# In the projections' stage of a two-layer trunk: rotation and weights' low parts from GpSimd to VectorE, decay weights and scan in fewer operations

## The chip, the cores and the metric

One core of one Trainium2 chip runs the whole kernel in one launch. The metric is device time in microseconds (us); the profile is one execution of the program, and its "span" is what the trace covers of it. Engines are named as in the profile: PE (TensorE), DVE (VectorE), ACT (ScalarE), POOL (GpSimd), SP (SyncE, which issues nearly all DMAs).

## The reference, cut to what matters

Two layers over 1024 latent tokens and 256 context tokens, D = 1024, all fp32. Each layer normalises and modulates its input, multiplies it by one wide input projection, and feeds three head groups: a Conformer convolution module, a bidirectional chunkwise retention and latent attention. Their outputs are concatenated, projected, and followed by a SwiGLU feed-forward part. The change lies in the retention and the latent heads' inputs:

```python
def _rotate_half_axis(x, pos):
    ...
    x1, x2 = xf[..., :f], xf[..., f:]
    return jnp.concatenate([x1 * cos - x2 * sin, x1 * sin + x2 * cos], axis=-1)

# retention, one chunk:
    o = einsum((q k^T) * dmat, v) + einsum(q, s) * xi
    s = s * g_chunk + einsum(k * zeta, v)
```

Retention's q and k (4 heads of 64) and the latent key's 32 rotary columns are rotated by row and column position, for the 1024 latent tokens only. The convolution has 31 taps over 256 channels.

## The kernel before, in words

Every fp32 matmul is done as three products of a high part (an fp32r rounding, made by ACT) and a low part (the difference, a subtraction in `split`, L80 through the helper `tt`): high by high, low by high, high by low. `piece` loads a 128x1024 piece of weights and splits it; unless told otherwise its low part is made on GpSimd.

The **projections' stage** comes once in each layer (about 146 to 412 us and 1832 to 2074 us of the span). Tokens go in ten tiles of 128: eight latent and two context. `load_chunk` splits the four pieces of a weight matrix, `project` runs 24 matmuls (eight k by three products) into one PSUM bank, and an evacuation follows. There are three passes over the tiles:

- **kv** (`evac_kv`): ACT copies the bank to `kv`, GpSimd rotates the key half (`rope_tm`: one 128x256 product, four 128x64 products, one 128x256 sum), the tile is stored to DRAM, and VectorE makes `kz`, the key times its decay weights in both directions (two operations). Four ticks later (`tk.later`; a tick is two k of a `project`, six matmuls) `states` multiplies `kz` by the values and ACT copies the result to `ST`. After the last tile a scan runs over the ten chunk states (`ST`, nine steps of four operations of 128x64, L660).
- **qg** (`evac_qg`): the same rotation for the query, then the gate (L672), `qx` (query times decay, two operations) and, some ticks later each, `ret_transposes`, `ret_scores` (VectorE multiplies by the decay mask: `AT`), `ret_values` (statistics on VectorE, the power on GpSimd: `rr`, L192) and `ret_store`. The second layer has no context tiles in this pass.
- **c** (`evac_cq`): the latent ranks. VectorE scales them, GpSimd rotates 32 columns, PE transposes them. Here too `conv_norm` normalises the convolution's output.

The 62 **taps** of the convolution (L584, `some_taps`) are VectorE operations of 128x1295 (first layer) or 128x1024 (second layer) elements, two chains of 31. They depend on nothing else in the stage, and only `conv_norm` needs their end. The program is scheduled by a planner that fills each engine's queue in order of emission among what is ready by its own estimate of times. So taps stand wherever VectorE was planned to be free. Once built, each engine's order is fixed: a late instruction holds up all that stand behind it on its engine.

The pools that matter: `kv` has two buffers, `qg` four, `kz` and `qx` share two, the rotation's `m1` and `m2` have one each, the table `rk` two, weights' `wh` and `wl` four each.

Of the kernel before, what the change touches and what calls it, by code (L numbers as in the profile page):

```python
# [11 lines left out]
F32 = mybir.dt.float32  # L12
# [9 lines left out]
T = 1024  # L22
# [6 lines left out]
H_RET = 4  # L29
# [14 lines left out]
def body(tc, I, out):  # L44
    nc = tc.nc
    mult, add, sub = ALU.mult, ALU.add, ALU.subtract
# [32 lines left out]
    def tt(out, a, b, op, eng=None):  # L79
        (eng or nc.vector).tensor_tensor(out=out, in0=a, in1=b, op=op)  # L80

    def split(h, l, t, heng=None, leng=None):

        if heng is None:
            nc.scalar.copy(h, t)  # L85
        else:
            heng.tensor_copy(h, t)
        tt(l, t, h, sub, leng)

    def load(src, n=1024):  # L90
        raw = rawp.tile([128, 1024], F32, name="raw", tag="raw")
        nc.sync.dma_start(out=raw[:, :n], in_=src)
        return raw

    def piece(src, n=1024, heng=None, leng=None, p=None, raw=None):

        raw = load(src, n) if raw is None else raw
        h = (p or whp).tile([128, 1024], F32R, name="wh", tag="wh", bufs=4)
        l = (p or wlp).tile([128, 1024], F32R, name="wl", tag="wl", bufs=4)
        split(h[:, :n], l[:, :n], raw[:, :n], heng, leng or nc.gpsimd)  # L100
        return h, l
# [35 lines left out]
    tk = Ticks()  # L137
# [333 lines left out]
    with ExitStack() as st:  # L471
# [26 lines left out]
        for k in range(KT):  # L498
            t = tp.tile([128, 512], F32, name="ht", tag="ht")
# [10 lines left out]
    for l in range(L):  # L510
# [31 lines left out]
        for g, (o, n) in enumerate(groups):  # L542
            for ct in range(2):
                pp = [bank("mm") for _ in range(2)]
                for hf in range(2):
                    for k in range(KT):
                        wh, wl = apcs[ct][k // 4]
                        c = (k % 4) * 256 + hf * 128
# [5 lines left out]
                        if k % 4 == 3 or k == 1:  # L554
# [4 lines left out]
                                               in1=pp[0][:, :n], op0=add, op1=mult)  # L559
# [11 lines left out]
        ST = rtp.tile([128, 10, 256], F32, name=f"ST{l}")  # L571
        dT, xi, zeta, gC = decay_tables(l, rtp)
        sp = sts.enter_context(pool(f"stage{l}", 2))
# [14 lines left out]
        taps = conv_taps()  # L588

        def load_chunk(name, ncol):  # L590
            return [piece(I[name][l, kp], 2 * ncol) for kp in range(4)]

        def project(pcs, ncol, t):

# [10 lines left out]
        def rope_tm(p, dst, tab, nh, f):  # L605

            w = 4 * f
            n = nh * w
            m1 = p.tile([128, 256], F32, name="m1", tag="m1", bufs=1)
            m2 = p.tile([128, 256], F32, name="m2", tag="m2", bufs=1)  # L610
            tt(m1[:, :n].rearrange("p (h w) -> p h w", h=nh), dst.rearrange("p (h w) -> p h w", h=nh),
               tab[:, 0:1, :].to_broadcast([128, nh, w]), mult, nc.gpsimd)
            sv = dst.rearrange("p (h b a f) -> p h b a f", h=nh, b=2, a=2)
            mv = m2[:, :n].rearrange("p (h b a f) -> p h b a f", h=nh, b=2, a=2)
            tv = tab[:, 1, :].rearrange("p (b a f) -> p b a f", b=2, a=2)
            for a in range(2):
                for b in range(2):
                    tt(mv[:, :, b, a, :], sv[:, :, b, 1 - a, :], tv[:, b:b + 1, a, :].to_broadcast([128, nh, f]), mult, nc.gpsimd)
            tt(dst, m1[:, :n], m2[:, :n], add, nc.gpsimd)


        fo = {**{t: t + 2 for t in LAT}, 8: 0, 9: 1}
# [3 lines left out]
        def by_head(a):  # L626
            return a.rearrange("p (h d) -> p h d", h=H_RET)

        def evac_kv(t, ps):
            kv = sp.tile([128, 512], F32, name="kv", tag="kv")  # L630
            if t < 8:
                nc.scalar.copy(kv, ps)
                tab = sp.tile([128, 2, 64], F32, name="rk", tag="rk")
                nc.sync.dma_start(out=tab, in_=I["rope_ret"][1, t])
                rope_tm(sp, kv[:, :256], tab, H_RET, 16)
            else:
                nc.scalar.activation(out=kv[:, :256], in_=ps[:, :256], func=AF.Copy, scale=0.125)
                nc.scalar.copy(kv[:, 256:], ps[:, 256:])
            if t in tiles:
                kvd[t] = drp.tile([128, 512], F32, name=f"kvd{l}{t}")  # L640
                nc.sync.dma_start(out=kvd[t], in_=kv)
            kz = sp.tile([128, H_RET, 2, 64], F32, name="kz", tag="kz")
            for i in range(2):
                tt(kz[:, :, i, :], by_head(kv[:, :256]), zeta[:, i, :].unsqueeze(2).to_broadcast([128, H_RET, 64]), mult)
            tk.later(4, states, t, kv, kz)

        def states(t, kv, kz):
            pu = bank("aux")
            for h in range(H_RET):
                nc.tensor.matmul(pu[:, h * 64:h * 64 + 64], lhsT=kz[:, h].rearrange("p a d -> p (a d)"),  # L650
                                 rhs=kv[:, 256 + h * 64:256 + h * 64 + 64], start=True, stop=True)
            if fo[t] < 9:
                nc.scalar.copy(ST[f_, fo[t] + 1, :], pu[f_, :256])
            if bo[t] < 9:
                nc.scalar.copy(ST[b_, bo[t] + 1, :], pu[b_, :256])
            if t == kvt[-1]:
                for i in range(9):
                    for h in range(H_RET):
                        c = slice(h * 64, h * 64 + 64)
                        nc.vector.scalar_tensor_tensor(out=ST[:, i + 1, c], in0=ST[:, i, c], scalar=gC[:, h:h + 1],  # L660
                                                       in1=ST[:, i + 1, c], op0=mult, op1=add)

        def evac_qg(t, ps):
            q = sp.tile([128, 512], F32, name="qg", tag="qg", bufs=4)
            nc.scalar.copy(q[:, :256], ps[:, :256])
            if t < 8:
                tab = sp.tile([128, 2, 64], F32, name="rk", tag="rk")
                nc.sync.dma_start(out=tab, in_=I["rope_ret"][0, t])
                rope_tm(sp, q[:, :256], tab, H_RET, 16)
            th = sp.tile([128, 256], F32, name="thg", tag="thg", bufs=1)  # L670
            nc.scalar.activation(out=th, in_=ps[:, 256:], func=AF.Tanh, scale=0.5)
            nc.vector.scalar_tensor_tensor(out=q[:, 256:], in0=th, scalar=1.0, in1=ps[:, 256:], op0=add, op1=mult)  # L672
            qx = sp.tile([128, H_RET, 2, 64], F32, name="qx", tag="kz")
            for i in range(2):
                tt(qx[:, :, i, :], by_head(q[:, :256]), xi[:, i, :].unsqueeze(2).to_broadcast([128, H_RET, 64]), mult)
            kv = sp.tile([128, 512], F32, name="kv2", tag="kv2", bufs=3)
            nc.sync.dma_start(out=kv, in_=kvd[t])
            tk.later(4, ret_transposes, t, q, qx, kv)
# [143 lines left out]
        for i, t in enumerate(kvt[2:]):  # L822
# [2 lines left out]
                if left:  # L825
                    tk.later(1 + 2 * j, conv_norm, left.pop(0))
            evac_cq(t, project(pcs, 416, t))
        wh, wl = piece(I["w_ukv"][l])
        wq = [piece(I["w_uq"][l, k]) for k in range(2)]
        vd = drp.tile([10, 128, 512], F32, name=f"vd{l}")  # L830

        def values(t_, p):
# [418 lines left out]
        for i, t in enumerate(order):  # L1251
# [8 lines left out]
            x = load_x(w2, t)  # L1260
# [106 lines left out]
        if last:  # L1367
            c = slice(0, 256)
# [8 lines left out]
            c = slice(256, 512)  # L1377
# [4 lines left out]
        else:  # L1382
            c = slice(0, 512)
# [16 lines left out]
        for j in range(NJ):  # L1400
            v = steps.pop(j) if j in steps else first_two(j)
            w, x, u, th1 = v.w, feat.op, v.u, v.th
# [133 lines left out]
        while ahead:  # L1536
            k, n, m, (a_, (bh, bl)) = ahead.pop(0)
            if not last and n in (0, 1, 2, 3):
                ch, cl = ctx[k]
                for t in CTX:  # L1540
                    if n in (0, 1):
                        cps[t] = bank("cx")
                    for i in range(m):
                        c, d, q = slice((t - 8) * 128, (t - 8) * 128 + 128), slice(i * 512, i * 512 + 512), 2 * i + n // 2
# [18 lines left out]
            for t in range(4):  # L1563
                ps = bank("po")
                for i in range(m):
                    c, d = slice(i * 512 + t * 128, i * 512 + t * 128 + 128), slice(i * 512, i * 512 + 512)
# [32 lines left out]
        for t in tiles:  # L1599
# [8 lines left out]
            for i, hf in inner:  # L1608
                wh, wl = pcs[i]
                d = slice(hf * 512, hf * 512 + 512)  # L1610
# [10 lines left out]
            x = load_x(e3, t)  # L1621
# [17 lines left out]
def _tables():  # L1639

    row, col = np.arange(T) // 64, np.arange(T) % 64

    def tab(f):
        cr, sr = _rope(row, f)
        cc, sc = _rope(col, f)
        return np.concatenate([cr, cr, cc, cc], 1), np.concatenate([-sr, sr, -sc, sc], 1)

    c16, s16 = tab(16)
    c8, s8 = tab(8)
    ret = np.stack([c16, s16], 1).reshape(8, 128, 2, 64)  # L1650
    rope_ret = np.stack([ret, ret * np.float32(0.125)])
    rope_kr = np.stack([c8, s8], 1).reshape(8, 128, 2, 32)
    rope_q = np.stack([np.tile(c8.T, (4, 1)), np.tile(s8.T, (4, 1))], 1) * np.float32(SCALE)
    m, c = np.arange(128)[:, None], np.arange(128)[None, :]
    posd = np.stack([np.maximum(c - m, 0), np.maximum(m - c, 0)], 1)
    p = np.arange(128)
    posc = np.stack([p + 1, 128 - p, 127 - p, p], 1)
    fold = np.array([[1, 0], [0, 1], [1, 1]])
    return {k: np.ascontiguousarray(v, dtype=np.float32) for k, v in
            dict(rope_ret=rope_ret, rope_kr=rope_kr, rope_q=rope_q, posd=posd, posc=posc, fold=fold).items()}  # L1660
# [67 lines left out]
```

## Time and profile before

| | us |
|---|---|
| median of three runs | 3169.01 (3164.75 to 3169.87) |
| profiled execution, its time | 3160.68 |
| span of its trace | 3158.9 |
| kv pass, qg pass, c pass of layer 1 in the trace | 146 to 225, 225 to 333, 333 to 412 |
| kv pass, qg pass, c pass of layer 2 | 1832 to 1910, 1910 to 1993, 1993 to 2074 |

How to read it: the profiled execution is one run, 8.3 us under the median of the three timed ones. A table of windows gives, for a stretch of the span, the busy time of each engine; PEclk is the granted clock of TensorE, 1.00 at 2.4 GHz and 0.50 at 1.2 GHz. A list of waits gives whom an engine waited for.

### The profile page before, as it was taken

Reading aid. Unit: us, or ns where it says so; the run is one execution under the profiler, and the core shown is the slowest. Engines: PE = TensorE matmul, PEld = TensorE weight load, DVE = VectorE, ACT = ScalarE, POOL = GpSimd, SP = SyncE. Lnnn points to the kernel's source line nnn. Section 1 sums busy time; section 2 is a strip of 40 time slices with the busy share of each in tenths; the row PEclk is TensorE's granted clock in tenths of the full one; section 3 lists DMA queues with packets and bytes.
Section 4 is the critical chain, followed back from the end, with each engine's and each line's share of the span. In section 5 each row is a group of like instructions: output and inputs, shape, how many; then the busy total and the mean of one; then the engine's idle time right before and its main releaser. Section 6 shows DMA issues by size and latency. Waiting matters only on the chain. (4 is left out here: it accounts for less than half of the span.)

```text
span 3158.9 us, 39704 instructions
## 1 busy us (share of the span) xinstructions
PE 2932.1 (93%) x13968; PEld 2275.9 (72%) x13968; DVE 2306.9 (73%) x3246; ACT 1194.4 (38%) x2354; POOL 1490.8 (47%) x1187
## 2 busy tenths in 40 slices
PE   7989989999889999999898898989999899999997
PEld 3667865567678888887776676875568678887785
DVE  4388568868897766655888868468957976666998
ACT  4223545653422222224332513545544322224432
POOL 1174435644332333226675375436654433334993
PEclk9999999999999999999999999989999999999998
DMA  7421157768522322223303421158864232224213
GB/s 276 143 66 38 46 189 179 179 160 270 172 77 92 105 92 92 98 71 131 112 21 110 153 66 48 44 175 194 198 193 139 97 114 89 82 83 155 98 62 120
DMA packets 178527, 381.47 MB, mean 121 GB/s; under 512 B 43255, under 2 KB 77687, under 8 KB 178072
## 3 DMA queue, kind: packets, MB, share of 16 engines
q1 hardware_dynamic: 172980, 360.03, 37.3%
q10 hardware_dynamic: 5348, 18.90, 1.5%
q8 instruction: 111, 1.82, 0.2%
q14 instruction: 88, 0.72, 0.1%
HBM read 242.97 MB, written 76.90 MB: 101 GB/s over the span
## 5 line engine op out<-in xcount | busy, mean ns | idle before, releaser
L80 POOL TENSOR_TENSOR wl<-raw,wh 128x512 fp32r<-128x512 f32 (+2 forms) x208 | 387.8, 1876 | 657.0 <-ACT wh L85 655.3
L85 ACT CAST wh<-raw 128x512 fp32r<-128x512 f32 (+2 forms) x305 | 237.4, 796 | 412.5 <-PE pp L105 192.9
L80 DVE TENSOR_TENSOR w<-pp,w 128x512 f32<-128x512 f32 x308 | 207.6, 686 | 189.2 <-PE pp L105 187.2
L105 PE MATMUL po<-wh,gh 128*128 128x512 f32 x504 | 203.1, 403 | 34.8 <-DVE p L80 28.2
L990 DVE TENSOR_REDUCE nm<-S 128x1 f32<-128x1280 f32 x128 | 189.7, 1482 | 56.1 <-PE S L105 54.7
L1003 ACT ACTIVATE P<-S,nm 128x1280 f32<-128x1280 f32 x120 | 159.4, 1329 | 176.0 <-DVE nm L990 175.8
L80 POOL TENSOR_TENSOR rr<-rv,mh 128x1 f32<-128x1 f32 (+2 forms) x130 | 93.2, 718 | 275.2 <-DVE rv L190 262.6
L1030 POOL COPY PT<-T 32x1280 f32<-32x1280 f32 x120 | 149.8, 1249 | 117.4 <-PE mm L1015 79.6
L105 PE MATMUL po<-wh,gl 128*128 128x512 f32 x504 | 200.3, 397 | 0.0
L105 PE MATMUL po<-wl,gh 128*128 128x512 f32 x504 | 200.0, 397 | 0.0
L584 DVE SCALAR_TENSOR_TENSOR cacc<-cy,cw,cacc 128x1295 f32<-128x1295 f32 (+1 forms) x120 | 190.1, 1625 | 0.0
L80 POOL TENSOR_TENSOR gl<-gr,gh 128x512 fp32r<-128x512 f32 x112 | 173.9, 1577 | 27.5 <-ACT gh L85 25.8
L80 POOL TENSOR_TENSOR wl<-sx,wh 128x1024 fp32r<-128x1024 f32 x44 | 108.4, 2464 | 157.4 <-ACT wh L85 137.2
L1095 DVE STREAM_TRANSPOSE T<-P 128x1280 f32<-128x1280 f32 x120 | 179.9, 1499 | 0.0
L80 DVE TENSOR_TENSOR raw<-raw 128x512 f32<-128x512 f32 (+1 forms) x96 | 128.2, 1344 | 51.9 <-POOL wl L80 48.5
L1041 PE MATMUL po<-PT,vr 128*64 128x512 f32 x600 | 155.7, 615 | 8.9 <-DVE raw L80 2.2
L105 PE MATMUL S<-kh,qh 96*128 96x512 f32 (+1 forms) x384 | 155.8, 406 | 6.4 <-ACT P L1003 4.4
L80 DVE TENSOR_TENSOR p<-p,po 128x512 f32<-128x512 f32 x224 | 145.3, 677 | 16.6 <-PE po L105 16.1
L105 PE MATMUL S<-kh,ql 96*128 96x512 f32 (+1 forms) x384 | 144.6, 376 | 11.1 <-POOL ql L80 11.0
L105 PEld LDWEIGHTS po<-wh,gh 128*128 128x128 f32 x504 | 97.2, 193 | 65.1 <-DVE p L80 33.2
L80 DVE TENSOR_TENSOR wl<-raw,wh 128x512 fp32r<-128x512 f32 (+1 forms) x105 | 124.4, 1194 | 26.4 <-ACT wh L85 25.0
L105 PE MATMUL S<-kl,qh 96*128 96x512 f32 (+1 forms) x384 | 142.8, 372 | 0.0
(438 smaller groups left out, 8723.6 us busy)
## 6 DMA issues: line engine op xcount, KB each, us to landing
PT<-T SPq DMA_DIRECT2D x360, 160.0 KB
raw<-in_mod_w SPq DMA_DIRECT2D x96, 512.0 KB
raw<-in_ffn_in SPq DMA_DIRECT2D x88, 512.0 KB
gd<-w SPq DMA_DIRECT2D x88, 256.0 KB
gr<-gd SPq DMA_DIRECT2D x32, 512.0 KB
xs<-x ACTq DMA_DIRECT2D x28, 512.0 KB
raw<-in_ffn_out SPq DMA_DIRECT2D x28, 512.0 KB
x<-xs SPq DMA_DIRECT2D x26, 512.0 KB
```

The source lines that it names most:

```text
L80: (eng or nc.vector).tensor_tensor(out=out, in0=a, in1=b, op=op)
L85: nc.scalar.copy(h, t)
L105: nc.tensor.matmul(ps, lhsT=a, rhs=b, start=start and i == 0, stop=stop and i == len(xs) - 1)
L584: nc.vector.scalar_tensor_tensor(out=acc[:, ct, :], in0=y0[:, ct, j:j + AW], scalar=w, in1=acc[:, ct, :], op0=mult, op1=add)
L990: nc.vector.reduce_max(out=u.nm, in_=ps[:, :nk], axis=AX.X, negate=True)
L1003: nc.scalar.activation(out=P, in_=u.ps, func=AF.Exp, bias=u.nm, accum_out=u.sm)
L1030: nc.gpsimd.tensor_copy(o, i)
L1041: nc.tensor.matmul(u.po[64 * (j % 2):64 * (j % 2) + 64], lhsT=u.hd.v[:, j, :], rhs=src[:, :, j * 32:j * 32 + 32], start=j < 2, stop=j > 7)
L1095: nc.vector.transpose(out=T1[:, :, u.a // 128].rearrange("p c (k i) -> p k c i", i=32), in_=u.P.rearrange("p (k c i) -> p k c i", c=4, i=32))
```

## The change

The rotation is done on VectorE in four operations: the source times the cosines, the source times the sines (whose halves are stored swapped in the table), and two sums, one for each half, that take the other half of the second product. It serves kv, qg and, with 32 columns, the c pass. The low parts of `w_kv`, `w_qg`, `w_c`, `w_ukv` and `w_uq` are made on VectorE; all other pieces stay. `kz` and `qx` are one operation of 512 elements each instead of two of 256. The scan's nine steps have two operations of 256 elements each instead of four of 64. `kv` shares the four buffers of `qg`, `kz` gets three, and `states` comes five ticks later instead of four.

```diff
         def load_chunk(name, ncol):
-            return [piece(I[name][l, kp], 2 * ncol) for kp in range(4)]
+            return [piece(I[name][l, kp], 2 * ncol, leng=nc.vector) for kp in range(4)]
...
-            tt(m1[:, :n].rearrange("p (h w) -> p h w", h=nh), dst.rearrange("p (h w) -> p h w", h=nh),
-               tab[:, 0:1, :].to_broadcast([128, nh, w]), mult, nc.gpsimd)
...
+            for i, m in enumerate((m1, m2)):
+                tt(m[:, :n].rearrange("p (h w) -> p h w", h=nh), dst.rearrange("p (h w) -> p h w", h=nh),
+                   tab[:, i:i + 1, :].to_broadcast([128, nh, w]), mult)
+            o, x, y = (a.rearrange("p (g a f) -> p g a f", a=2, f=f) for a in (dst, m1[:, :n], m2[:, :n]))
             for a in range(2):
-                for b in range(2):
-                    tt(mv[:, :, b, a, :], sv[:, :, b, 1 - a, :], tv[:, b:b + 1, a, :].to_broadcast([128, nh, f]), mult, nc.gpsimd)
-            tt(dst, m1[:, :n], m2[:, :n], add, nc.gpsimd)
+                tt(o[:, :, a], x[:, :, a], y[:, :, 1 - a], add)
...
-            kv = sp.tile([128, 512], F32, name="kv", tag="kv")
+            kv = sp.tile([128, 512], F32, name="kv", tag="qg", bufs=4)
...
-            kz = sp.tile([128, H_RET, 2, 64], F32, name="kz", tag="kz")
-            for i in range(2):
-                tt(kz[:, :, i, :], by_head(kv[:, :256]), zeta[:, i, :].unsqueeze(2).to_broadcast([128, H_RET, 64]), mult)
-            tk.later(4, states, t, kv, kz)
+            kz = sp.tile([128, H_RET, 2, 64], F32, name="kz", tag="kz", bufs=3)
+            tt(kz, by_head(kv[:, :256]).unsqueeze(2).to_broadcast([128, H_RET, 2, 64]),
+               zeta.rearrange("p i h -> p h i").unsqueeze(3).to_broadcast([128, H_RET, 2, 64]), mult)
+            tk.later(5, states, t, kv, kz)
...
+                g = gC.unsqueeze(2).to_broadcast([128, H_RET, 64])
                 for i in range(9):
-                    for h in range(H_RET):
-                        c = slice(h * 64, h * 64 + 64)
-                        nc.vector.scalar_tensor_tensor(out=ST[:, i + 1, c], in0=ST[:, i, c], scalar=gC[:, h:h + 1],
-                                                       in1=ST[:, i + 1, c], op0=mult, op1=add)
+                    d = sp.tile([128, 256], F32, name="sd", tag="thg", bufs=1)
+                    tt(by_head(d), by_head(ST[:, i, :]), g, mult)
+                    tt(ST[:, i + 1, :], ST[:, i + 1, :], d, add)
...
-        wh, wl = piece(I["w_ukv"][l])
-        wq = [piece(I["w_uq"][l, k]) for k in range(2)]
+        wh, wl = piece(I["w_ukv"][l], leng=nc.vector)
+        wq = [piece(I["w_uq"][l, k], leng=nc.vector) for k in range(2)]
...
+    def halves_swapped(s):
+        return s.reshape(T, 2, 2, -1)[:, :, ::-1].reshape(s.shape)
...
-    ret = np.stack([c16, s16], 1).reshape(8, 128, 2, 64)
+    ret = np.stack([c16, halves_swapped(s16)], 1).reshape(8, 128, 2, 64)
```

`qx` is changed as `kz` is, and `rope_kr` as `ret` is.

## Rows read from the trace of the kernel before

**Rows 1.** The page's part 1: busy us, share of the span, instructions of each engine.

```profile
PE 2932.1 (93%) x13968; PEld 2275.9 (72%) x13968; DVE 2306.9 (73%) x3246; ACT 1194.4 (38%) x2354; POOL 1490.8 (47%) x1187
```

**Rows 2.** Windows: start:end, us, busy PE, PEld, DVE, ACT, POOL, then PEclk, DMA.

```profile
148.00:320.00 172.00, 151.20 (x748) 121.44 (x746) 144.86 (x220) 44.24 (x109) 108.23 (x108) 0.93 0.18 55
1835.00:1969.00 134.00, 117.40 (x571) 94.16 (x569) 116.57 (x173) 32.11 (x77) 87.45 (x86) 0.95 0.18 57
320.00:367.00 47.00, 45.07 (x285) 40.52 (x286) 22.09 (x78) 27.25 (x85) 20.01 (x37) 1.00 0.20 60
```

**Rows 3.** Waits of PE, 140 to 430 us: us in total, times, longest.

```profile
PE aux L650 <- DVE kz L80: 8.3, 5, 2.5
PE mm L105 <- POOL wl L80: 5.7, 4, 1.9
PE rx L686 <- DVE qx L80: 3.6, 1, 3.6
...
PE ry L683 <- DVE AT L80: 2.1, 3, 1.3
```

**Rows 4.** Waits of PE, 1815 to 2110 us, same columns.

```profile
PE aux L650 <- DVE kz L80: 9.4, 4, 2.6
PE aux L781 <- DVE cq L769: 6.3, 4, 3.5
PE ry L683 <- DVE AT L80: 5.9, 4, 2.8
...
PE mm L105 <- POOL wl L80: 3.3, 2, 1.6
```

**Rows 5.** Timeline of POOL in the kv pass: start, us, instructions.

```profile
198.38 6.69 POOL L80 TENSOR_TENSOR m<-kv,rk 128x256 f32<-128x256 f32 x5 [1.09 <-issue]
```

**Rows 6.** Windows, columns of Rows 2: a PE gap, then stretches at half clock.

```profile
204.80:207.30 2.50, 0.04 (x1) 0.00 (x0) 1.39 (x3) 0.58 (x1) 2.34 (x4) 0.95 0.31 113
...
176.30:179.70 3.40, 3.40 (x11) 2.82 (x11) 3.40 (x3) 0.73 (x2) 3.40 (x3) 0.51 0.34 82
207.10:213.90 6.80, 6.56 (x20) 5.53 (x21) 5.78 (x7) 0.73 (x2) 5.63 (x5) 0.50 0.13 44
251.40:258.20 6.80, 6.80 (x24) 5.24 (x22) 4.27 (x6) 1.89 (x5) 1.38 (x4) 0.50 0.00 0
...
1862.50:1865.90 3.40, 3.40 (x9) 2.66 (x8) 3.25 (x3) 0.21 (x1) 3.32 (x3) 0.50 0.29 88
1900.10:1903.50 3.40, 3.40 (x11) 2.82 (x11) 3.40 (x6) 0.76 (x2) 0.00 (x0) 0.50 0.00 1
1920.60:1927.30 6.70, 6.59 (x20) 5.56 (x21) 6.70 (x18) 1.14 (x3) 4.26 (x4) 0.50 0.03 10
...
2115.10:2142.40 27.30, 27.30 (x73) 20.56 (x73) 23.33 (x17) 13.51 (x19) 14.35 (x11) 0.50 0.67 153
```

**Rows 7.** DVE's groups by shape, 148 to 320 us: busy, mean ns, idle before.

```profile
L584 DVE SCALAR_TENSOR_TENSOR cacc<-cy,cw,cacc 128x1295 f32<-128x1295 f32 x59 | 101.2, 1751 | 0.0
L80 DVE TENSOR_TENSOR kz<-kv,zeta 128x256 f32<-128x256 f32 x20 | 11.3, 608 | 10.4 <-POOL kv L80 10.4
L660 DVE SCALAR_TENSOR_TENSOR ST<-ST,gC 128x64 f32<-128x64 f32 x36 | 9.4, 336 | 0.0
```

**Rows 8.** DVE's groups by shape, 1835 to 1969 us, same columns.

```profile
L584 DVE SCALAR_TENSOR_TENSOR cacc<-cy,cw,cacc 128x1024 f32<-128x1024 f32 x60 | 87.3, 1503 | 0.0
```

**Rows 9.** Instructions on cacc, then kz: ns min/median/max, starts, forms.

```profile
L584 DVE SCALAR_TENSOR_TENSOR cacc<-cy,cw,cacc x120: 1251/1560/3704, 152.0 to 1967.6; 128x1295 f32<-128x1295 f32 x60, 128x1024 f32<-128x1024 f32 x60
...
L80 DVE TENSOR_TENSOR kz<-kv,zeta x40: 412/426/2562, 158.7 to 1920.0; 128x256 f32<-128x256 f32 x40
```

**Rows 10.** DVE elsewhere: a 128-element product (timeline); 512 elements; low parts (groups).

```profile
701.09 0.28 DVE L80 TENSOR_TENSOR od<-od,S 64x128 f32<-64x128 f32 x1 [3.79 <-ACT od L1087]
...
L80 DVE TENSOR_TENSOR w<-pp,w 128x512 f32<-128x512 f32 x308 | 207.6, 686 | 189.2 <-PE pp L105 187.2
...
L80 DVE TENSOR_TENSOR wl<-raw,wh 128x1024 fp32r<-128x1024 f32 x52 | 68.7, 1320 | 12.1 <-ACT wh L85 10.7 <-POOL m_l L80 1.4
```

More of the change, by code (lines that the diff above doesn't have):

```diff
@@ L610, in rope_tm @@
             m2 = p.tile([128, 256], F32, name="m2", tag="m2", bufs=1)
-            tt(m1[:, :n].rearrange("p (h w) -> p h w", h=nh), dst.rearrange("p (h w) -> p h w", h=nh),
-               tab[:, 0:1, :].to_broadcast([128, nh, w]), mult, nc.gpsimd)
-            sv = dst.rearrange("p (h b a f) -> p h b a f", h=nh, b=2, a=2)
-            mv = m2[:, :n].rearrange("p (h b a f) -> p h b a f", h=nh, b=2, a=2)
-            tv = tab[:, 1, :].rearrange("p (b a f) -> p b a f", b=2, a=2)
+            for i, m in enumerate((m1, m2)):
+                tt(m[:, :n].rearrange("p (h w) -> p h w", h=nh), dst.rearrange("p (h w) -> p h w", h=nh),
+                   tab[:, i:i + 1, :].to_broadcast([128, nh, w]), mult)
+            o, x, y = (a.rearrange("p (g a f) -> p g a f", a=2, f=f) for a in (dst, m1[:, :n], m2[:, :n]))
             for a in range(2):
-                for b in range(2):
-                    tt(mv[:, :, b, a, :], sv[:, :, b, 1 - a, :], tv[:, b:b + 1, a, :].to_broadcast([128, nh, f]), mult, nc.gpsimd)
-            tt(dst, m1[:, :n], m2[:, :n], add, nc.gpsimd)
+                tt(o[:, :, a], x[:, :, a], y[:, :, 1 - a], add)
         fo = {**{t: t + 2 for t in LAT}, 8: 0, 9: 1}
@@ L672, in evac_qg @@
             nc.vector.scalar_tensor_tensor(out=q[:, 256:], in0=th, scalar=1.0, in1=ps[:, 256:], op0=add, op1=mult)
-            qx = sp.tile([128, H_RET, 2, 64], F32, name="qx", tag="kz")
-            for i in range(2):
-                tt(qx[:, :, i, :], by_head(q[:, :256]), xi[:, i, :].unsqueeze(2).to_broadcast([128, H_RET, 64]), mult)
+            qx = sp.tile([128, H_RET, 2, 64], F32, name="qx", tag="kz", bufs=3)
+            tt(qx, by_head(q[:, :256]).unsqueeze(2).to_broadcast([128, H_RET, 2, 64]),
+               xi.rearrange("p i h -> p h i").unsqueeze(3).to_broadcast([128, H_RET, 2, 64]), mult)
             kv = sp.tile([128, 512], F32, name="kv2", tag="kv2", bufs=3)
@@ L1646, in tab @@
         return np.concatenate([cr, cr, cc, cc], 1), np.concatenate([-sr, sr, -sc, sc], 1)
+    def halves_swapped(s):
+        return s.reshape(T, 2, 2, -1)[:, :, ::-1].reshape(s.shape)
     c16, s16 = tab(16)
     c8, s8 = tab(8)
-    ret = np.stack([c16, s16], 1).reshape(8, 128, 2, 64)
+    ret = np.stack([c16, halves_swapped(s16)], 1).reshape(8, 128, 2, 64)
     rope_ret = np.stack([ret, ret * np.float32(0.125)])
-    rope_kr = np.stack([c8, s8], 1).reshape(8, 128, 2, 32)
+    rope_kr = np.stack([c8, halves_swapped(s8)], 1).reshape(8, 128, 2, 32)
     rope_q = np.stack([np.tile(c8.T, (4, 1)), np.tile(s8.T, (4, 1))], 1) * np.float32(SCALE)
```

## The prediction

> **What bounds the kernel now.** I read the page's busy times first: TensorE is busy 93% of the span, VectorE 73%, GpSimd 47% [rows 1]. So time is saved where PE stands still or runs slowly, and an edit on another engine counts only through that. Next come windows over the stage, from the first tap of the convolution to the last: 172 us in the first layer, 134 us in the second. PE is idle for 172 - 151.2 = 20.8 us and 134 - 117.4 = 16.6 us of them, at a mean granted clock of 0.93 and 0.95, while VectorE is busy 144.9 and 116.6 us [rows 2].
>
> The waits of PE say for whom it stood. For the key's decay weights (`kz`, L650): 8.3 and 9.4 us. For low parts made on GpSimd: 5.7 and 3.3. For `qx` behind the scan: 3.6, first layer. For `AT` in the retention: 2.1 and 5.9 [rows 3, 4]. `kz` is late because VectorE itself waited 10.4 us for GpSimd's rotated tile [rows 7], and five products of one rotation took 6.7 us there [rows 5]. VectorE stands with its whole queue in such a wait: its order is fixed, and taps behind a waiting `kz` don't move.
>
> The clock windows show a second price. In the gap from 204.8 to 207.3 PE did nothing for 2.5 us; from 207.1 to 213.9 it had 0.50, that is 1.2 GHz. Six such stretches in the two kv passes and starts of the qg passes last 3.4 + 6.8 + 6.8 + 3.4 + 3.4 + 6.7 = 30.5 us [rows 6]. At half speed each loses half its length of matmul work: 15.2 us.
>
> **The change part by part.**
>
> *Rotation of kv.* GpSimd loses six operations per latent tile, VectorE gains four. A 256-element product costs 0.42 us (median of `kz`, same operands) [rows 9], a 128-element one 0.28 [rows 10]: 2 x 0.42 + 2 x 0.28 = 1.4 us against 6.7 and more. No row shows VectorE on runs of 16 elements, as the sums have; I bound a sum by 0.28 below and by 0.42, a full tile's price, above (1.7 us a rotation), and take 0.28, since it has that element count. `kz` follows in the same queue with no wait on another engine. A tap in progress can hold it by up to 1.56 us [rows 9], but `states` now comes one tick, six matmuls, later, and four buffers instead of two keep ACT from waiting for a free `kv`. I take all of the `kz` waits away: 8.3 + 9.4 = **17.7 us**. Ends: nothing (a tap always in the way) and 17.7.
>
> *Low parts.* A piece on VectorE costs 1.32 us [rows 10]. The four `w_kv` pieces fall where taps have not begun, `w_qg` and `w_c` among taps. The waits for GpSimd's low parts go, 5.7 + 3.3 = **9.0 us**; a wait for ACT's high part would be next, and so would a tap ahead of a piece (ends 0 and 9.0).
>
> *Scan and decay weights.* `kz` goes from 2 x 0.608 to one operation of 512 elements, 0.69 [rows 7, 10]; the scan from 9.4 us to 18 x 0.42 = 7.6 us [rows 7, 9]. With `states` one tick later, the scan also comes after the first query tile's evacuation, so `qx` no longer stands behind it: **3.6 us** [rows 3], ends 0 and 3.6.
>
> *Rotation of qg.* It takes the waits for GpSimd out of VectorE's queue, ahead of `AT`, but puts 1.4 us in. Of the 2.1 + 5.9 = 8.0 us for `AT` [rows 3, 4] I give a third back, **2.7 us**; ends: a loss of 8.0 and a gain of 8.0.
>
> *Clock.* If the gaps go, so does most of what follows them. I take three quarters of 15.2: **11.4 us** (ends 0 and 15.2); some gaps of the retention will still throttle.
>
> *VectorE's account.* First layer, 148 to 320 us: 16 rotations of 1.4 and four pieces of 1.32 add 27.7; `kz` saves 11.3 - 10 x 0.69 = 4.4, the scan 1.8. Net +21.5 on 144.9. But a tap takes 1.75 us on average there, 1.56 as a median [rows 7, 9]. I put the difference down to GpSimd reading beside it, and it goes when GpSimd falls silent: 59 x 0.19 = 11.3 us. Left: 155.1 of 172 us, 90%. Second layer, with the same net: 116.6 + 21.5 - 60 x (1.503 - 1.251) = 123.0 of 134 [rows 2, 8, 9]. This cover is thin inside the stretch, but taps are fillers and may run later: from 320 to 367 us VectorE is busy only 22.1 of 47 us [rows 2], and nothing needs the taps before `conv_norm`. If that cover went, the first rival below would hold.
>
> *The c pass.* The 32-column rotation (eight tiles) and three pieces (4.0 us a layer) join a VectorE on which PE already waits: 6.3 us for `cq` in the second layer [rows 4]. Ends: nothing, and that wait doubled in both layers, 12.6. I take **5 us** lost, as VectorE is idle half of the time just before it [rows 2].
>
> *Taps in the way.* Each of 38 kv and qg tiles (20 + 18) may wait up to a tap, 1.56 us: ends 0 and 59. Most have ticks to spare; I take a twelfth, **5 us**.
>
> *Queues.* No DMA is added. SP's stores of `kvd` and loads of `rk` behind them waited for GpSimd's rotation and now wait for a VectorE that ends it sooner; GpSimd's queue keeps only the powers (`rr`), which no longer stand behind rotations. At nothing: both queues run beside PE's matmuls, and if SP were late, the next weight piece would be.
>
> **Sum.** 17.7 + 9.0 + 3.6 + 2.7 + 11.4 - 5 - 5 = 34.4 us. Profiled execution: 3160.7 - 34.4 = 3126.3 us. It lies 8.3 us under the median of the three runs, so against that median, 3169.0, the forecast is **3135 us**.
>
> **The rivals.**
>
> *A. VectorE sets the pace up to the last tap* (no change, or little). For: 90% and 92% by the account above. Its idle time now is 27.1 us (first layer), of which only the 10.4 for `kz` certainly goes; if half of the other 16.7 stays, the stretch takes 155.1 + 8.4 = 163.5, a gain of 8.5. Second layer: idle 17.4, half stays: 131.7, a gain of 2.3. Less 5 for the c pass: about 6 us, **3163 us**. Against: the planner puts taps behind what is due, and they can slide past 320 us. Chance 0.14.
>
> *B. Slower: the rotation stands in front of `AT`.* Place: VectorE's queue in the qg pass, where PE's fixed order waits for each tile's `AT` and `z`. Price: rotation 1.4 and a tap 1.56, 3.0 us a tile, 18 tiles: 54 us lost. Gained on the kv side: 17.7 + 9.0 + three quarters of half of 23.7 us at half clock (all six but the one at 251.4), 8.9. Less 5: 54 + 5 - 35.6 = 23 us slower, **3192 us**. It decides from a lateness of (35.6 - 5) / 18 = 1.7 us a tile on. For: PE waits for `AT` already today [rows 3, 4]. Against: VectorE loses its waits for the rotated query, and a rotation belongs to a tile whose transposes are due four ticks later. Chance 0.08. The Trainium skill (Perfetto Trace Analysis, Identifying the Most-Contended Engine) has a rule on this side: improve the engine with the highest occupancy first; the change loads VectorE, which has the higher occupancy of the two it concerns. By that rule alone the sum would be the account's net, some 20 us a layer lost; the waits of PE, mostly for GpSimd's work, speak against it here.
>
> *C. More than forecast.* From 2115 to 2142 us PE runs 27.3 us at half clock [rows 6], at the door of the second layer's attention. If the stage ends otherwise, that may vanish too: 13.6 us more, about **3121 us**. Against: a gap just ahead of it is none that the change touches. Chance 0.14.
>
> That the change does not do what it says is hardly a case: engine, shape and count of each operation are given.
>
> **How the numbers follow.** Forecast 0.64, with its own range of 3122 to 3150 from the ends of clock, `AT` and tap costs; A 0.14, B 0.08, C 0.14. The time is that of the likeliest case. The range reaches to C below, with some of the upper ends of the gains (3110), and to A above (3164); left out are B, half of A, and little below. About 0.2% (6 us) is what a measurement can tell from no change: half of A lies within it. Faster: 0.64 + 0.14 + 0.07 = 0.85; same 0.07; slower 0.08.
>
> **What would show it.** Right: PE's waits for `kz` and for low parts nearly absent; kv pass shorter by 10 to 15 us in each layer; taps near 1.56 and 1.25 us on average; fewer than three half-clock stretches in kv and qg together; GpSimd nearly empty there. A shows as a VectorE without idle time and a first `conv_norm` that waits for the last tap; B as PE's waits for `AT` and `z` above 30 us. Rotations above 2 us each would make the account wrong, and with it the forecast.

## The result, and the profile after

The change makes the kernel **81 us faster**: 3087.89 us (3084.57 to 3096.54, four runs) against 3169.09, a ratio of 0.9753 [0.9739, 0.9767] (in brackets a 95% interval, here and below). The direction was forecast, the size was not: the gain is more than twice the 34.4 us of the sum, and the time lies below the range. The profiled execution has a span of 3082.8 us, 76.1 less than before; it lies 3.3 us under its own median, the one of before 8.3 under its own, and 76.1 + 8.3 - 3.3 = 81.1. All executions compared here have a mean granted clock of 0.96 to 0.98; one of an added-work kernel below, at 0.567 and 4722.68 us, is left out.

Part 1 of the page after answers to [rows 1]:

```profile
PE 2896.8 (94%) x13968; PEld 2252.0 (73%) x13968; DVE 2318.9 (75%) x3394; ACT 1196.4 (39%) x2354; POOL 1240.9 (40%) x869
```

VectorE carries only 12 us more than before, though GpSimd has given up 250. PE's own busy time fell by 35 us with the same 13968 matmuls, and its mean granted clock rose from 0.969 to 0.979.

Where the time went is read best between events that both kernels have. These windows run from ACT's first copy of a `kv` tile to its last copy of a `qg` tile, and from there to the last copy of a transposed key at the end of the c pass, for both layers; columns as in [rows 2]. Before:

```profile
152.70:332.40 179.70, 159.16 (x813) 128.72 (x813) 147.56 (x236) 53.53 (x130) 110.02 (x110) 0.93 0.18 55
332.40:445.80 113.40, 104.92 (x567) 90.55 (x566) 59.53 (x164) 55.79 (x172) 48.57 (x90) 0.97 0.35 117
1838.40:1992.10 153.70, 135.69 (x697) 109.52 (x696) 122.81 (x204) 44.83 (x106) 97.56 (x102) 0.96 0.17 54
1992.10:2104.90 112.80, 100.22 (x529) 86.72 (x529) 56.51 (x152) 52.54 (x163) 49.03 (x92) 0.97 0.33 109
```

And after:

```profile
148.40:291.90 143.50, 143.50 (x810) 120.18 (x808) 132.38 (x259) 53.55 (x130) 10.08 (x7) 1.00 0.22 69
291.90:404.80 112.90, 104.07 (x572) 88.54 (x572) 77.20 (x211) 56.20 (x172) 31.85 (x37) 1.00 0.34 115
1799.10:1923.30 124.20, 124.20 (x689) 104.10 (x687) 114.89 (x228) 45.47 (x106) 6.38 (x5) 1.00 0.20 65
1923.30:2030.40 107.10, 99.51 (x538) 84.83 (x538) 68.54 (x200) 52.84 (x163) 26.38 (x33) 1.00 0.34 114
```

In kv and qg PE is now busy in every microsecond by the profile, at full clock (1.00): 143.50 of 143.50 and 124.20 of 124.20. The two stretches are 36.2 and 29.5 us shorter, the c passes 0.5 and 5.7. With the 4.3 us by which the first window starts earlier, less 1.7 given back between the layers, plus 1.6 after the last window, that is the 76.1.

PE's waits from 140 to 430 us, and (after the dots) from 1765 to 2040, columns as in [rows 3]:

```profile
PE S L105 <- ACT P L1000: 3.1, 3, 1.3
PE ry L792 <- DVE cz L799: 2.9, 7, 1.1
PE ry L792 <- DVE cacc L584: 1.4, 1, 1.4
PE aux L778 <- DVE cq L766: 1.4, 3, 0.6
...
PE ry L792 <- DVE cz L799: 2.2, 5, 0.9
PE aux L778 <- DVE cq L766: 1.7, 2, 0.9
...
PE ry L680 <- DVE AT L80: 0.4, 1, 0.4
```

All that [rows 3, 4] showed for `kz`, low parts, `qx` and `AT` is gone but 0.4 us. What is left belongs to the c pass and the attention. Line 3 is the last tap: the first `conv_norm` waited 1.4 us for it.

VectorE's groups from 144 to 292 us answer to [rows 7]:

```profile
L584 DVE SCALAR_TENSOR_TENSOR cacc<-cy,cw,cacc 128x1295 f32<-128x1295 f32 x49 | 76.3, 1560 | 0.1
L80 DVE TENSOR_TENSOR kz<-kv,zeta 128x512 f32<-128x512 f32 x10 | 6.9, 686 | 1.6 <-ACT kv L634 1.4
...
L80 DVE TENSOR_TENSOR m<-kv,rk 128x256 f32<-128x256 f32 x16 | 6.1, 421 | 0.9 <-ACT kv L629 0.9
L80 DVE TENSOR_TENSOR wl<-raw,wh 128x1024 fp32r<-128x1024 f32 x5 | 6.0, 1219 | 0.2 <-ACT wh L85 0.2
...
L80 DVE TENSOR_TENSOR kv<-m,m 128x128 f32<-128x128 f32 x16 | 3.9, 284 | 0.0
```

A tap takes 1.56 us instead of 1.75, a product of the rotation 0.42, a sum on runs of 16 elements 0.28, and the 10.4 us that VectorE stood for GpSimd's tile are gone. This window holds ten taps fewer than that of [rows 7] (49 against 59): they slid behind 292 us.

### The profile page after: what moved, and what is told of

It reads as the page before. It is cut to its first block, busy times and chain, and to the rows that moved or that the text cites. A ratio compares the mean times of both kernels' runs of the same rounds, so it can differ in the third digit from the quotient of the medians.

```text
span 3082.8 us, 39513 instructions
## 1 busy us (share of the span) xinstructions
PE 2896.8 (94%) x13968; PEld 2252.0 (73%) x13968; DVE 2318.9 (75%) x3394; ACT 1196.4 (39%) x2354; POOL 1240.9 (40%) x869
## 5 line engine op out<-in xcount | busy, mean ns | idle before, releaser
L80 POOL TENSOR_TENSOR wl<-raw,wh 128x512 fp32r<-128x512 f32 (+1 forms) x178 | 310.9, 1758 | 550.1 <-ACT wh L85 550.0
L105 PE MATMUL po<-wh,gh 128*128 128x512 f32 x504 | 203.3, 403 | 33.5 <-DVE p L80 24.4
L80 DVE TENSOR_TENSOR wl<-raw,wh 128x1024 fp32r<-128x1024 f32 (+2 forms) x135 | 158.9, 1185 | 46.7 <-ACT wh L85 46.7
L584 DVE SCALAR_TENSOR_TENSOR cacc<-cy,cw,cacc 128x1295 f32<-128x1295 f32 (+1 forms) x120 | 169.5, 1419 | 0.2
L1331 ACT ACTIVATE w<-w 128x512 f32<-128x512 f32 x88 | 55.6, 632 | 220.3 <-DVE w L80 220.3
```

The lines of the kernel that those rows point to most:

```text
L105: nc.tensor.matmul(ps, lhsT=a, rhs=b, start=start and i == 0, stop=stop and i == len(xs) - 1)
L584: nc.vector.scalar_tensor_tensor(out=acc[:, ct, :], in0=y0[:, ct, j:j + AW], scalar=w, in1=acc[:, ct, :], op0=mult, op1=add)
L1331: nc.scalar.activation(out=th, in_=u, func=AF.Tanh, scale=0.5)
```

## The experiments

The texts quoted below name theories by letters. **W**: GpSimd's long rotations make PE's gaps, directly and through VectorE's fixed queue, and the half clock comes behind the gaps. **L**: the low parts are a cause of their own. **S**: the buffers and the later tick are what helps. **P** and **Q**: the small edits matter in combination. **A**: VectorE paces the stage. **C**: GpSimd's work beside VectorE slows both (contention). **D**: only the lateness of GpSimd's results counts.

**One part alone.** First the rotation only, on the kernel of before:

```diff
-            tt(m1[...], dst[...], tab[:, 0:1, :]..., mult, nc.gpsimd)
...
+            for i, m in enumerate((m1, m2)):
+                tt(m[...], dst[...], tab[:, i:i + 1, :]..., mult)
...
+                tt(o[:, :, a], x[:, :, a], y[:, :, 1 - a], add)
```

> Only the rotation moves to VectorE (four operations); low parts, buffers, ticks, decay weights and scan as before. Theory W (PE's gaps come from GpSimd's long rotations, directly and through VectorE's fixed queue, and each gap brings half clock behind it): 45 to 60 us faster than before, PE's waits for kz and AT under 4 us in each layer, taps near 1.56 us on average, and PE's waits for GpSimd's low parts (5.7 and 3.3 us) left. Rival S (kz was late because kv has two buffers and states comes a tick too early): 10 to 25 us faster, kz waits still over 5 us a layer. Rival L (the low parts were the main cost): under 20 us.

Measured: 0.9878 [0.9858, 0.9899], 39 us. PE's waits from 140 to 430 us:

```profile
PE mm L105 <- POOL wl L80: 4.3, 4, 1.9
...
PE aux L647 <- DVE kz L80: 1.3, 1, 1.3
```

`kz` is down from 8.3 to 1.3 [rows 3], the low parts still cost 4.3. The two kv and qg windows are 25.8 and 17.1 us shorter and the c passes 2.8 and 0.7 longer. W's mechanism is there, with less gain than W asked, and one of its signs failed: the mean tap is 1.658 us in the first layer, not near 1.56, and 1.478 in the second, hardly below the 1.503 of before [rows 8]. The low parts still on GpSimd account for much of that. VectorE's and GpSimd's groups by shape from 1874 to 1889 us:

```profile
L584 DVE SCALAR_TENSOR_TENSOR cacc<-cy,cw,cacc 128x1024 f32<-128x1024 f32 x6 | 15.8, 2694 | 0.0
L80 POOL TENSOR_TENSOR wl<-raw,wh 128x1024 fp32r<-128x1024 f32 x4 | 12.6, 3176 | 56.6 <-ACT wh L85 56.6
```

Beside four low parts six taps take 2.69 us each, against a mean of 1.277 in the kernel after, though no tap needs a low part.

Then the low parts only:

```diff
-            return [piece(I[name][l, kp], 2 * ncol) for kp in range(4)]
+            return [piece(I[name][l, kp], 2 * ncol, leng=nc.vector) for kp in range(4)]
...
-        wh, wl = piece(I["w_ukv"][l])
+        wh, wl = piece(I["w_ukv"][l], leng=nc.vector)
```

> Only the low parts of the stage's weights move to VectorE; rotation stays on GpSimd. Theory W: 10 to 20 us faster (9.0 us of waits, and the half clock at 207 and 1921 us in part); kz waits stay at 8 to 10 us a layer. Rival S: the same 10 to 15. Rival L: 40 us or more.

Measured: 0.9898 [0.988, 0.9916], 34.5 us: far more than W allowed, less than L's 40, and nearly four times the 9.0 us that PE had waited for low parts [rows 3, 4]. Waits from 140 to 430 us:

```profile
PE aux L650 <- DVE kz L80: 6.2, 4, 2.5
PE ry L683 <- DVE AT L80: 4.2, 2, 2.4
...
PE mm L105 <- DVE wl L80: 0.9, 1, 0.9
```

With the rotation still on GpSimd `kz` fell from 8.3 to 6.2, and the mean tap of each layer from 1.747 and 1.503 us to 1.616 and 1.360. So a low part on GpSimd cost more than the wait that bears its name; the six taps above show one way. That GpSimd's rotations no longer queue behind low parts is another, which this run does not separate.

Buffers and tick only:

```diff
-            kv = sp.tile([128, 512], F32, name="kv", tag="kv")
+            kv = sp.tile([128, 512], F32, name="kv", tag="qg", bufs=4)
...
-            tk.later(4, states, t, kv, kz)
+            tk.later(5, states, t, kv, kz)
```

> Only kv's four buffers, kz's three and states one tick later; rotation and low parts stay on GpSimd. Theory W: 5 to 20 us faster; GpSimd's kv rotations take 5 to 7.5 us beside the taps, about the pace of a tile, so kz is still late at times (kz waits 2 to 6 us a layer). Rival S: 30 us or more faster, kz waits gone.

Measured: 0.9975 [0.9961, 0.999], 10 us by the medians. PE's waits for `kz` stay, 9.9 and 8.6 us, where W had put 2 to 6. S falls as the main cause.

Decay weights in one operation and scan in two, only:

```diff
-                    for h in range(H_RET):
...
+                    tt(by_head(d), by_head(ST[:, i, :]), g, mult)
+                    tt(ST[:, i + 1, :], ST[:, i + 1, :], d, add)
```

> Only decay weights in one operation and the scan in two per step. Theory W: 2 to 8 us faster (VectorE's work falls by some 6 us a layer, but it waits for GpSimd all the same; the wait for qx behind the scan, 3.6 us, shrinks by 1.8). A rival by which the number of VectorE's operations paces the stage: 15 us or more.

Measured: 1.0063 [1.0038, 1.0087], **21 us slower**, against expectation. Two views tell why, first PE's longest wait from 140 to 430 us, then VectorE in the scan (timeline: start, us, instructions):

```profile
PE aux L713 <- ACT stt L693: 8.2, 1, 8.2
```

```profile
260.60 1.55 DVE L584 SCALAR_TENSOR_TENSOR cacc<-cy,cw,cacc 128x1295 f32<-128x1295 f32 x1
262.08 0.41 DVE L80 TENSOR_TENSOR ST<-ST,sd 128x256 f32<-128x256 f32 x1
265.01 0.69 DVE L80 TENSOR_TENSOR qx<-qg,xi 128x512 f32<-128x512 f32 x1 [2.52 <-POOL qg L80]
265.62 0.42 DVE L80 TENSOR_TENSOR sd<-ST,gC 128x256 f32<-128x256 f32 x1
265.96 1.56 DVE L584 SCALAR_TENSOR_TENSOR cacc<-cy,cw,cacc 128x1295 f32<-128x1295 f32 x1
267.43 0.42 DVE L80 TENSOR_TENSOR ST<-ST,sd 128x256 f32<-128x256 f32 x1
```

Each of the nine steps is a chain of two operations that depend on each other, and the planner put a tap between them where it could; three `qx` that wait for GpSimd's query tile stand there too, for 1.02, 1.58 and 2.52 us. The scan's nine sums lie between 236.9 and 267.9 us, where the old scan took 9.4 us in one piece [rows 7]. PE stands 8.2 us for a state that it needs; the second layer has the same wait with 5.6 us. Windows of the gap and of what follows it:

```profile
260.10:268.40 8.30, 0.42 (x2) 0.00 (x0) 5.78 (x9) 0.86 (x3) 3.84 (x6) 0.84 0.03 8
268.40:275.20 6.80, 6.45 (x22) 5.78 (x23) 5.14 (x16) 2.25 (x6) 0.88 (x1) 0.50 0.14 39
```

After 8.3 us with 0.42 us of matmul PE works at half clock.

**The whole change with one part undone.** The old scan back (four operations a step), then the old buffers and tick, then the c pass's rotation and its three pieces back on GpSimd:

```diff
-                    tt(by_head(d), by_head(ST[:, i, :]), g, mult)
-                    tt(ST[:, i + 1, :], ST[:, i + 1, :], d, add)
+                    for h in range(H_RET):
...
```

> The changed kernel with the scan of before (36 operations of 128x64, four independent ones a step). Seen so far: the two-operation scan alone, without the rest, lets the planner put a tap between any two of its dependent operations; it stretched from 9 to 31 us, and PE waited 8.2 us for a chunk state. Theory W: in the changed kernel PE is without a gap there, so the old scan changes it by under 5 us either way against 3087.9 us (3083 to 3093). Rival Q (the slow scan still costs in the combination): 8 us or more faster, under 3080.

```diff
-            tk.later(5, states, t, kv, kz)
+            tk.later(4, states, t, kv, kz)
...
```

> The changed kernel with two buffers for kv, two for kz and states four ticks later, as before. Alone these three gave 10 us. Theory W: the rotation on VectorE is short, so they give under 8 us here: 3088 to 3096. Rival S (they are what lets the parts add up to more than their sum): 3100 us or more, with waits for kz or for a chunk state.

```diff
-                rope_tm(sc, cq[:, 384:], tab, 1, 8)
+                rope_tm(sc, cq[:, 384:], tab, 1, 8, nc.gpsimd)
...
-        wh, wl = piece(I["w_ukv"][l], leng=nc.vector)
+        wh, wl = piece(I["w_ukv"][l])
```

> The changed kernel with the c pass's part undone: the 32-column rotation and the low parts of w_ukv and w_uq are back on GpSimd. The prediction put this part at 5 us lost; then this kernel would be 3080 to 3086. Theory W2 (it gains, since the powers on GpSimd no longer stand behind rotations and low parts): 3 to 8 us slower than the changed kernel, 3091 to 3096.

Measured: 0.9764 [0.9742, 0.9785], 0.9758 [0.9738, 0.9778], 0.9762 [0.9738, 0.9786]. None differs from the whole change. Q falls, and so does S in the combination. The c pass's part stays open: at that width 5 us lost or 3 to 8 gained cannot be told apart. Then rotation and low parts together, with nothing else changed (the two diffs above):

> Rotation and low parts moved to VectorE, nothing else of the change. Alone they gave 39 and 35 us. If buffers, tick, one-operation decay weights and scan matter only where something else is late (theory W): 3083 to 3094 us, as the whole change. Rival P (the whole is more than these two because of the small edits together): 3098 or more.

Measured: 0.9758 [0.974, 0.9776], the whole gain. P falls. The four parts alone add up to 39 + 34.5 + 10 - 21 = 62.5 us of 81; the two that matter, 39 + 34.5 = 73.5 of the 79 of both together. The interleaved scan that cost 21 us alone costs nothing in the whole: it runs from 213 to 230 us there, with no `qx` behind GpSimd in it, and PE has no wait for a state.

**Does VectorE pace the stage?** On the whole change, two more 256-element products on VectorE for each of the 32 rotated kv and qg tiles, to no use (0.76 us a tile, 24 us in both layers together):

```diff
+            if n == 256:
+                for _ in range(2):
+                    tt(m1[...], dst[...], tab[:, 0:1, :]..., mult)
```

> The changed kernel with two more 256-element products on VectorE for each rotated tile of kv and qg (their result is overwritten or not used in a way that leaves out part of the rotation's value for m1 only in time: the same product is written again): 0.76 us a tile, 32 tiles, 24 us of VectorE's time. Theory W (VectorE has room, taps slide): 0 to 6 us slower than the changed kernel, up to 3094. Rival A (VectorE sets the pace): 20 us or more slower, 3108 or more.

Measured: 0.9813 [0.9788, 0.9839], some 16 us over the three kernels above, on the same chip. Once more, for its trace:

> The changed kernel with two more products a rotated tile on VectorE again, for its trace (the one before was disturbed): about 3106 us. If VectorE sets the pace: no idle time on it from first to last tap, the last tap moves to where conv_norm waits for it, and PE's waits lie at AT, z and the first conv_norm. If the extra products only lengthen the rotation's chain: waits for kz and qx.

Measured: 0.9768 [0.9749, 0.9788], 3098.45 us against 3092.84 for rotation and low parts on the same chip. Its windows, cut at the same events:

```profile
147.90:292.60 144.70, 143.82 (x808) 120.13 (x807) 132.33 (x283) 53.76 (x130) 9.14 (x7) 1.00 0.22 68
292.60:414.20 121.60, 107.71 (x574) 91.58 (x573) 88.18 (x219) 57.10 (x173) 31.68 (x37) 0.96 0.32 109
1805.40:1930.90 125.50, 124.93 (x686) 104.09 (x686) 115.65 (x250) 45.11 (x106) 5.36 (x5) 1.00 0.20 64
1930.90:2040.80 109.90, 100.25 (x540) 84.84 (x540) 78.26 (x210) 53.18 (x164) 27.28 (x33) 1.00 0.33 111
```

kv and qg are 1.2 and 1.3 us longer, the c passes 8.7 and 2.8. VectorE's busy time in kv and qg did not rise (132.33 against 132.38): taps made room, 42 of them stand before 292 us where 49 did, and the later ones hold up the c pass. So load that the planner knows of slides; these windows give 14 us for 24, the two comparisons of whole times, of the same kernel, 16 (near A's 20) and 6 (W's upper end). A is half right: VectorE's slack in the stage seems nearly used up, but the change did not run into it.

**Does GpSimd's work cost time when nobody waits for it?** On the whole change, six 256-element products on GpSimd for each rotated tile, of a constant tile with itself, into a buffer that nobody reads (computation added):

```diff
+            if n == 256:
+                gs_ = p.tile([128, 256], F32, name="gs_", tag="gs_", bufs=1)
+                for _ in range(6):
+                    tt(gs_..., side..., side..., mult, nc.gpsimd)
```

> The changed kernel with GpSimd multiplying a constant tile into a scratch tile, six 128x256 products for each rotated tile, some 70 us a layer; nobody reads or waits for them. They add to the computation and take nothing from it. Theory C (half of the gain is that GpSimd's reads no longer slow VectorE): taps 1.65 us or more on average in the first layer, 10 to 30 us slower than the changed kernel. Rival D (only the rotation's length and the queue behind it mattered): taps as slow, but the time within 5 us of 3088.

Measured: 0.9836 [0.9821, 0.9851]; 3120.77 us against 3092.84 for rotation and low parts (the whole gain) on the same chip, **28 us lost to work that no instruction waits for**. D falls. C's time came, and its taps nearly: 1.63 us on the mean in the first layer, 1.45 in the second. Its windows of kv and qg:

```profile
149.70:303.50 153.80, 147.25 (x808) 122.62 (x807) 143.10 (x258) 53.26 (x129) 41.01 (x34) 0.98 0.20 64
...
1806.40:1953.90 147.50, 134.70 (x687) 110.79 (x686) 139.83 (x229) 44.95 (x105) 75.73 (x68) 0.93 0.17 55
```

The idle products are done early: eleven of the first layer's sixteen sets of six ran before its kv pass. So the two layers are two doses: 41.01 - 10.08 = 30.9 us of GpSimd's work more made the first window 10.3 us longer, 75.73 - 6.38 = 69.4 us more the second 23.3: 0.33 and 0.34 us for each. PE's only wait there is the one that the change had removed, first from 140 to 310 us, then from 1790 to 1960:

```profile
PE aux L655 <- DVE kz L80: 6.5, 3, 3.4
...
PE aux L655 <- DVE kz L80: 12.8, 6, 3.0
```

How VectorE came to be late is plain in its timeline (start, us, instructions), first in this run:

```profile
159.16 1.09 DVE L80 TENSOR_TENSOR kz<-kv,zeta 128x512 f32<-128x512 f32 x1
160.18 1.58 DVE L80 TENSOR_TENSOR m<-kv,rk 128x256 f32<-128x256 f32 x2
161.68 1.91 DVE L584 SCALAR_TENSOR_TENSOR cacc<-cy,cw,cacc 128x1295 f32<-128x1295 f32 x1
163.52 0.90 DVE L80 TENSOR_TENSOR kv<-m,m 128x128 f32<-128x128 f32 x2
```

and in the kernel after:

```profile
158.98 0.69 DVE L80 TENSOR_TENSOR kz<-kv,zeta 128x512 f32<-128x512 f32 x1
...
161.09 0.76 DVE L80 TENSOR_TENSOR m<-kv,rk 128x256 f32<-128x256 f32 x2
161.77 1.56 DVE L584 SCALAR_TENSOR_TENSOR cacc<-cy,cw,cacc 128x1295 f32<-128x1295 f32 x1
163.25 0.49 DVE L80 TENSOR_TENSOR kv<-m,m 128x128 f32<-128x128 f32 x2
```

The same four: 0.69 to 1.09, 0.76 to 1.58, 1.56 to 1.91, 0.49 to 0.90 us. Nothing waits; every operation is longer, and the queue behind them is late.

**The six kernels in one table**, GpSimd's busy time in the kv and qg window beside the window's length, layer 1 and layer 2 (us):

| | POOL 1 | length 1 | POOL 2 | length 2 |
|---|---|---|---|---|
| before | 110.0 | 179.7 | 97.6 | 153.7 |
| buffers and tick | 115.7 | 177.3 | 99.0 | 151.9 |
| low parts | 93.1 | 168.4 | 80.1 | 149.6 |
| GpSimd beside | 41.0 | 153.8 | 75.7 | 147.5 |
| rotation | 27.7 | 153.9 | 27.8 | 136.6 |
| after | 10.1 | 143.5 | 6.4 | 124.2 |

The length falls with GpSimd's work, but not at one price. The rotation alone lies above the rest: what is left on GpSimd there is mostly low parts, and they cost 10.4 us for 17.6 and 12.4 for 21.4, 0.59 and 0.58 us a microsecond. PE waits for the low parts themselves there, and they slow the taps most. At the idle products' 0.335 us a microsecond the 99.9 and 91.2 us taken from GpSimd would give 33.5 and 30.5 against the 36.2 and 29.5 measured. That is an estimate, and its closeness may be chance: the idle products are another mix of operations. It does not divide the gain, since a rotation on GpSimd makes VectorE both slower and wait [rows 7], and no run here has a rotation on GpSimd that does only one of them. How much of the 66 us each is worth stays open.

## Why the prediction was right in direction and wrong in size

**The step that failed is the price of a part: PE's waits for that part's own product, a share of the half clock listed behind them, and a charge for loading VectorE.** I let GpSimd's slowing of VectorE enter only VectorE's own account, as 11.3 us of taps that buy room, and put it at nothing in PE's time. The runs show it there: idle products on GpSimd cost 28 us and bring waits for `kz` back, and the low parts, priced at 9.0, give 34.5 alone. In the sum the waits themselves are near, since they were read from PE whatever made them late. What was put behind and beside them is off: the two charges for VectorE, the half clock, and time at full clock that had no term. How much of each row below is GpSimd's slowing is not shown. Term by term, in the windows above:

| | forecast | measured |
|---|---|---|
| PE idle in kv and qg (`kz` 17.7, low parts 9.0, `qx` 3.6, `AT` 2.7) | 33.0 | 38.6 |
| half clock there | 11.4 | 18.7 |
| busy time at full clock in the same two windows | none | 8.5 |
| c pass | -5 | +6.2 |
| taps in the way | -5 | 0 |
| start of the stage and the rest | none | 4.2 |
| sum (the measured column up to rounding) | 34.4 | 76.1 |

- **Waits.** 20.5 and 18.0 us of idle in the two windows, all gone: `kz` 17.7, low parts 8.6, `qx` 3.6, `AT` 7.2, and 1.5 for ACT's copy of `kv`, which had no term. `kz` and low parts went as put. `AT` was mis-sized: I gave a third back, and all but 0.4 us of it went, probably since VectorE's queue ahead of `AT` no longer holds a wait for GpSimd's query tile.
- **Where in the stage.** I expected the kv pass 10 to 15 us shorter. From ACT's first copy of a `kv` tile to that of the last context tile it is 14.9 and 13.7, as put. Another 5.3 and 3.4 came from there to the first query tile, and 15.9 and 12.5 in the qg pass, where I had put little.
- **Clock.** Three quarters of what I listed was too few: none of the stretches in these windows is left, and my list lacked one of 6.8 us at 299 us, in the qg pass. 3.4 + 3 x 6.8 = 23.8 and 3.4 + 3.4 + 6.7 = 13.5 us at 0.50, half of it 18.7.
- **Not booked at all.** Less idle and half clock, before has 147.3 and 128.9 us of matmul time in these windows, after 143.5 and 124.2 for the same work. PE stands 14 and 12 times in these windows of before, so some price at the edge of a gap suggests itself; it was not tried, and the ends of matmuls are modelled.
- **The c pass.** It did not lose 5 us but gained 6.2, with clock 1.00 instead of 0.97 and PE waiting 1.4 and 1.7 us for `cq` instead of 2.6 and 6.3. The charge thus had the wrong sign, but why is not shown. With the c pass's part back on GpSimd it is 2.9 and 3.8 us longer than after; rotation and low parts alone, which have that part on VectorE, are 2.5 and 0.2 longer, so at most the second layer says something, and in the whole time nothing shows.
- **Taps in the way.** No wait in kv or qg shows one, though the planner set a tap between the two halves of a rotation.
- **VectorE's account** held in its prices: the taps came out at 1.560 and 1.277 us against 1.56 and 1.25 put, a rotation at 0.76 + 0.49 = 1.25 against 1.4, and VectorE is busy 132.4 of 143.5 and 114.9 of 124.2, 92% in both layers, against 90 and 92 put for the old stretches. The shares agree by luck in part, since ten taps left the first window and it shrank with them.
- **Rivals.** A had its sign, one wait of 1.4 us for the last tap, without its price; the added products show that it begins not far beyond. B's wait is 0.4 us (and its price counted a rotation for 18 query tiles, where 16 are rotated). C's mechanism came: 27.3 us at half clock at the attention's door [rows 6] became 10.2. Its price did not: from the first score maximum there to the end only 1.6 us were gained, so the half clock there was no 13.6 us to be had. The Trainium skill's rule (Perfetto Trace Analysis, Identifying the Most-Contended Engine), improve the engine with the highest occupancy first, taken for the two engines that the change concerns, points away from it: VectorE's occupancy rose from 73 to 75%, and the time fell by 81 us.

## What to carry to other kernels

Before an engine is credited with work "beside" another, look at the other's instructions: where their mean lies above their median, that can be a cost (idle work added beside them tells), and in a tightly ordered queue the late results reach TensorE under the slowed engine's name. Price a gap in TensorE with the half clock behind it, and list every half-clock stretch of the stage before taking a share. Splitting a dependent chain into fewer, larger operations can lengthen it if a scheduler puts fillers between them.

## What the runs showed of the hardware

GpSimd and VectorE slow each other, both ways. The idle products take 0.61 us each while VectorE is quiet, and 1.0 to 1.3 in the mean beside it. Two rows of that run, first of GpSimd's groups by shape from 1802 to 1880 us, then of GpSimd's timeline before the stage (start, us for all six with the gaps between them):

```profile
L80 POOL TENSOR_TENSOR gs__16258<-side 128x256 f32<-128x256 f32 x6 | 7.6, 1264 | 0.5
```

```profile
96.85 4.08 POOL L80 TENSOR_TENSOR gs__1192<-side 128x256 f32<-128x256 f32 x6 [16.96 <-DVE side L606]
```

A tap went from 1.56 to 1.91 us, a 256-element product from 0.42 to 0.83 in layer 2's kv pass, `kz` from 0.69 to 1.06. The same products for the query, made when the idle ones were over, took 0.42. Low parts slow more: with the rotation alone moved, six taps beside four of them took 2.69 us each instead of 1.28, and a low part 3.18 instead of the 2.39 of one made before the taps began. In the kernel before, two taps beside low parts took 3.67 and 3.65 us (from 225.21 us on), close to the longest of all, 3.70 [rows 9].

The Trainium skill (SBUF — State Buffer, Who interferes with whom) says that a VectorE instruction with two inputs in SBUF contends with a GpSimd instruction that reads SBUF. The traces agree: the operations named all have two inputs. The Trainium skill (SBUF — State Buffer, SBUF: two separate sides) says that the one that starts first keeps the ports for its whole instruction and the other is blocked. Of that the traces show the size alone: a tap grew by 0.35 us beside products of 0.61, and by 1.4 us beside low parts of 2.39.

I had not expected that load and slowness differ so. 24 us of VectorE work that the planner knew of cost 2.5 us in kv and qg, since taps moved out; the slowness, 10.7 and 24.9 us of VectorE's busy time in the two windows, came through as 10.3 and 23.3 us.
